# Two changes in a two-block transformer kernel: part of the mixer's convolution as diagonal matmuls, and a reordered front

## The chip, the cores and the metric

One core of one Trainium2 chip runs the whole program. The metric is the device time of one execution in microseconds (us); a lower time is better. The times shown are medians over runs of the same kernel, and one further execution was profiled.

## The reference

Two transformer blocks follow one another on 512 tokens of width 1024, all in float32. The first block has a modulation from a condition vector `c`, two attention branches of eight heads (stick breaking and forgetting) and gates. The second block adds a hybrid mixer, a cross attention to a memory of 256 rows, and a feed-forward part. What matters here is the mixer and the memory:

```python
    q, k, v, u = split(h @ w_in)                 # 512, 512, 512 and 1024 columns
    a = diff_attention(rope(q), rope(k), v)      # 4 heads, two score maps each
    a = rmsnorm(a, subln_g) * (1.0 - lam_init)
    c = u[..., :512] * sigmoid(u[..., 512:])     # the gated unit
    c = causal_dwconv(c, cv_dw_w) + cv_dw_b      # 31 taps for each of 512 channels
    c = silu(layernorm(c, cv_ln_g, cv_ln_b))
    return concat(a, c) @ w_out
    ...
    m = rmsnorm(mem, norm_mem_g)                 # 256 x 1024
    kv = m @ w_ckv                               # keys and values of the cross attention
```

## The kernel before, in words

Activations lie feature-major, 128 features on the partitions and 512 tokens along the row. Weights are stored as units of 128 x 1024 floats (512 KB). `unit` (L150) loads one on SP's queue into one of three `wr` tiles, ScalarE copies it to a rounded `wh` (L146), and VectorE or GpSimd writes the remainder `wl` (L147). Which of the two does it is set by a string: "D" is VectorE, "P" is GpSimd, and "DP" alternates. The strings are `START_LO`, `B1_LO`, `B2_LO` and so on; the list restarts at its first letter when a stage changes it. Each product is three matmuls (high times high, high times low, low times high, L153 to L156), with the moving operand 512 or 256 columns wide. `lin_k` (L158) runs one unit of eight blocks, so 24 matmuls; `tok` (L170) runs 48 matmuls of 256 columns for a unit.

PSUM has eight banks: three for `lin`, three for `z`, one for `pv` and one for `sm`.

The program is written as straight Python, but the order in which each engine gets its instructions is made by a scheduler of the framework. It takes the written order as a priority and moves work forward where its model finds an engine free and a buffer available. Every engine then works through its own queue in order, and so does each DMA queue.

**The front (L304 to L424).** `memory` (L314) loads the transposed memory (two transfers of 512 KB), scales and splits it, then loads the memory a second time by rows (`mem_n`, again two transfers of 512 KB), squares it on ScalarE with a row sum (L334), and from that makes the norm of the rows. Then a loop over eight `j` runs one unit of keys (`mem_k`, L338), two `ar` loads and multiply-sums for shift and scale (`ada`, L380, L384, 16 loads of 512 KB in four buffers), and after every second `j` two units of values (`mem_v`, L345). The four loads of `x` stand in the first pass, the norm of `x` (`row_norm`, L390) in the second: squares on ScalarE, column sums as matmuls with one column. At the end eight `h` tiles are made (L414 to L418), the inputs of all later products. The keys and values go to memory through GpSimd's DMA queue (L343, L363).

**The mixer (L760 to L1006).** The order is a string, `MIX` (L92), read at L966:

```python
MIX = "u0 u1 u2 u3 q0 f0 q1 f1 v1 v0 f3 b0 b1 c b3 f2 l b2"
```

`u` is the gated unit of 128 channels (`glu`, L768: two units of weights, products by `rb` on VectorE at L774 and L775, a sigmoid, a product on GpSimd at L777). `q` makes rotated queries and keys of two heads (`rotated`, L817, six small VectorE operations on each of two tiles, L830 to L835). `f` is the first half of a head (`diff_front`, L861: transposes at L842, scores, softmax), `b` the second (`diff_back`, L887: transposes at L492, the product with the values in `pv`, a norm). `v` makes values. `c` is the convolution of all four channel groups (`conv`, L908), `l` the layer norm (L941). For each of the four groups VectorE runs one `tensor_scalar` for tap 0 (L917) and 23 taps as `scalar_tensor_tensor` (L929), both tensor inputs in SBUF:

```python
dve.scalar_tensor_tensor(out=ca, in0=x_, scalar=w_, in1=ca, op0=ALU.mult, op1=ALU.add)
```

Seven taps go over ScalarE (a scaled copy, L922 and L925) and GpSimd (an addition, L926); L930 adds the two sums. After the mixer its output products `wo2c` (L988, the convolution's half) and `wo2a` (L996, the heads' half) follow.

Of the kernel before, what the change touches and what calls it, by code (L numbers as in the profile page):

```python
# [7 lines left out]
F32 = mybir.dt.float32  # L8
# [34 lines left out]
for _name, _n in (  # L43
# [4 lines left out]
):  # L48
    _add(_name, _n)
# [41 lines left out]
GLU_LO = "PPD"  # L91
MIX = "u0 u1 u2 u3 q0 f0 q1 f1 v1 v0 f3 b0 b1 c b3 f2 l b2"  # L92


@with_exitstack
def block_kernel(ctx, tc, wts, vec, c_row, lam_v, cst, x_t, mem_t, mem_n, pos, out):
    nc = tc.nc
# [210 lines left out]
    ms = []  # L310
    mrc = st.tile([P, 2], F32, name="mrc")
    mrb = st.tile([P, NM], F32, name="mrb")

    def memory():  # L314
        mem_r = mem_t.rearrange("(k p) m -> p k m", p=P)
        msum = st.tile([P, 2], F32, name="msum")
        for j in range(2):
            raw = st.tile([P, D], F32, tag="mr", bufs=4, name="mr")
            nc.sync.dma_start(out=raw.rearrange("p (k m) -> p k m", k=4), in_=mem_r[:, 4 * j:4 * j + 4])
            for a in range(2):  # L320
                hi, lo = htile(), htile()
                src = raw[:, a * T:(a + 1) * T]
                for e in range(2):
                    k = 4 * j + 2 * a + e
                    m = slice(e * NM, (e + 1) * NM)
                    g = V("g_mem", k)
                    act.activation(out=hi[:, m], in_=src[:, m], func=AF.Identity, scale=g)
                    dve.scalar_tensor_tensor(out=lo[:, m], in0=src[:, m], scalar=g, in1=f32(hi[:, m]),
                                             op0=ALU.mult, op1=ALU.subtract)
                    ms.append((hi[:, m], lo[:, m]))  # L330
        for i in range(2):
            raw = st.tile([P, D], F32, tag="mr", bufs=4, name="mr")
            nc.sync.dma_start(out=raw, in_=mem_n[i * P:(i + 1) * P])
            act.activation(out=raw, in_=raw, func=AF.Square, accum_out=msum[:, i:i + 1])  # L334
        rsq(mrc, msum, D)
        bcast(mrc, mrb, 2)

    def mem_k(c):  # L338
        o = ps_lin()
        lin_k(o[:, :NM], unit("mk", c), 0, ms)  # L340
        q = st.tile([P, NM], F32, tag="kvo", bufs=2, name="kvo")
        dve.tensor_tensor(out=q, in0=o[:, :NM], in1=mrb, op=ALU.mult)
        nc.gpsimd.dma_start(out=kv_d[c // 4, :, (c % 4) * NM:(c % 4 + 1) * NM], in_=q)  # L343

    def mem_v(h):  # L345
# [14 lines left out]
        for i in range(2):  # L360
            q = st.tile([P, NM], F32, tag="kvo", bufs=2, name="kvo")
            act.activation(out=q, in_=o[:, i * 256:(i + 1) * 256], func=AF.Copy, scale=mrc[:, i:i + 1])
            nc.gpsimd.dma_start(out=kv_d[2 + i, :, h * 256:(h + 1) * 256], in_=q)  # L363
# [13 lines left out]

    mod = st.tile([P, 2 * KD], F32, name="mod")

    def ada(j):  # L380
        for n, name in enumerate(("shift", "scale")):
# [6 lines left out]
                       bias=gain0[:, j:j + 1])  # L388

    def row_norm():  # L390
        cs = ps_sm()
        for k in range(KD):
            q = st.tile([P, T], F32, tag="xq", bufs=4, name="xq")
            act.activation(out=q, in_=xt0[:, k], func=AF.Square)
            for i in range(NT):
                mm(cs[:, i:i + 1], q[:, i * P:(i + 1) * P], ones[:, 0:1], k == 0 and i == 0, k == KD - 1)
        xrc = st.tile([P, NT], F32, name="xrc")
        rsq(xrc, cs[:, :NT], D)
        xrb = st.tile([P, T], F32, name="xrb")
        bcast(xrc, xrb)  # L400
        return xrb

    hs = []
    for j in range(KD):
        mem_k(j)
        if j == 0:
            for k in range(0, KD, 2):
                nc.sync.dma_start(out=xt0[:, k:k + 2], in_=x_t[k * P:(k + 2) * P].rearrange("(k p) t -> p k t", p=P))
        ada(j)
        if j == 1:  # L410
            xrb = row_norm()
        if j % 2:
            mem_v(j // 2)
    for j in range(KD):  # L414
# [3 lines left out]
        hs.append(split_sb(xk))  # L418
    csts = st.tile([P, D], F32, tag="ar", bufs=AR_BUFS, name="csts")
# [467 lines left out]
    def diff_back(h, pt, s0):  # L887
# [19 lines left out]

    def conv():  # L908
        for c in range(4):
            cp = cps[c]  # L910

            def tap(j):
                return cp[:, 30 - j:30 - j + T], V("cv_w", c * 31 + j)

            ca = b2p.tile([P, PADW], F32, tag="cp", bufs=CP_BUFS, name="ca")[:, :T]
            x_, w_ = tap(0)
            dve.tensor_scalar(out=ca, in0=x_, scalar1=w_, scalar2=V("cv_b", c), op0=ALU.mult, op1=ALU.add)  # L917
            cb_ = (rb[:, 1], nacc[:, 0])[c % 2]
            for j in range(1, 1 + CONV_POOL):
                x_, w_ = tap(j)  # L920
                if j == 1:
                    act.activation(out=cb_, in_=x_, func=AF.Copy, scale=w_)  # L922
                else:
                    pr = b2p.tile([P, T], F32, tag="cpr", bufs=2, name="cpr")
                    act.activation(out=pr, in_=x_, func=AF.Copy, scale=w_)  # L925
                    pool.tensor_tensor(out=cb_, in0=cb_, in1=pr, op=ALU.add)  # L926
            for j in range(1 + CONV_POOL, 31):
                x_, w_ = tap(j)
                dve.scalar_tensor_tensor(out=ca, in0=x_, scalar=w_, in1=ca, op0=ALU.mult, op1=ALU.add)  # L929
            dve.tensor_tensor(out=ca, in0=ca, in1=cb_, op=ALU.add)  # L930
            cacc.append(ca)
            if c == 1:
                csum.append(nacc[:, 1])
                pool.tensor_tensor(out=csum[0], in0=cacc[0], in1=ca, op=ALU.add)
            elif c == 2:
                pool.tensor_tensor(out=csum[0], in0=csum[0], in1=ca, op=ALU.add)

# [28 lines left out]
    for step in MIX.split():  # L966
# [203 lines left out]
def _layout(i):  # L1170
# [83 lines left out]
    for h in range(8):  # L1254
# [32 lines left out]
```

## Time and profile before

| | us |
|---|---|
| median of 3 runs | 1299.48 (1299.35 to 1299.97) |
| the profiled execution | 1301.97 |
| its span, from first to last instruction | 1300.0 |
| TensorE matmul busy | 1220.0 (94%) |
| TensorE weight load busy | 1035.3 (80%) |
| VectorE busy | 831.4 (64%) |
| ScalarE busy | 595.0 (46%) |
| GpSimd busy | 404.1 (31%) |

Engines: PE is TensorE's matmul, PEld its weight load, DVE VectorE, ACT ScalarE, POOL GpSimd, SP the queue that issues most DMAs. Busy shares are averages over stages with different limits. The granted clock (PEclk) is 1.00 at 2.4 GHz and 0.50 at 1.2 GHz. A line of the trace is often that of a helper, so the tile's name tells what it belongs to. Matmuls are pipelined: the mean duration of one is longer than the distance to the next, which is taken from how many start in a stretch.

### The profile page before, as it was taken

To read this page: it belongs to the slowest core of one execution; us is meant where nothing else is said; L and a number is where in the kernel's file an instruction comes from. 1 tells how busy PE (TensorE), PEld (TensorE's weight loads), DVE (VectorE), ACT (ScalarE), POOL (GpSimd) and SP (SyncE) were. 2 spreads that over 40 slices of the span, in tenths; PEclk is the share of its full clock that TensorE was granted. 3 is DMA by queue.
4 is the path that set the end of the run, shared out by engine and by line. 5 is a ranking of instruction groups with operands and counts; after the bars stand their busy time and mean duration, and the time that the engine had idled before them with its cause. 6 is when DMAs were issued, how large, how long until landed. Compare 5 with 4: busy or idle time off the path is not lost.

```text
span 1300.0 us, 16674 instructions
## 1 busy us (share of the span) xinstructions
PE 1220.0 (94%) x6310; PEld 1035.3 (80%) x6310; DVE 831.4 (64%) x1276; ACT 595.0 (46%) x985; POOL 404.1 (31%) x280
## 2 busy tenths in 40 slices
PE   6999999999999999986697799999999999999996
PEld 5899887988887888875595687887888888888886
DVE  5963777666466175699999757466587777771112
ACT  5743556456652236334445646444444444442221
POOL 0121543422221228456721018103422222223222
PEclk8999999999999999987896689999999999999998
DMA  9863232222247443221221014211333233322221
GB/s 362 287 218 99 74 98 73 66 82 89 66 138 247 139 125 109 86 65 49 73 58 41 9 49 146 83 49 56 106 98 98 97 97 98 98 89 89 92 87 65
DMA packets 43425, 134.85 MB, mean 104 GB/s; under 512 B 4945, under 2 KB 8529, under 8 KB 43346
## 3 DMA queue, kind: packets, MB, share of 16 engines
q1 hardware_dynamic: 42578, 131.69, 31.9%
q0 software_dynamic: 768, 2.10, 0.4%
q8 instruction: 50, 0.82, 0.2%
q14 instruction: 29, 0.24, 0.1%
HBM read 124.33 MB, written 6.29 MB: 100 GB/s over the span
## 4 chain that ended last, share of the span: by engine, by line
PE 77%; DVE 14%; ACT 4%; DMA 3%; issue 2%; POOL 1%; SPq 0%; DVEq 0%; ACTq 0%; POOLq 0%
PE lin L128 64%; PE z L128 6%; DVE ca L929 6%; PE pv L128 3%; DVE wl L147 1%; PE sm L128 1%; PE z L492 1%; DMA wr<-in_wts 1%; DVE h L200 1%; DVE xr L758 1%; DMA ar<-in_wts 1%; DMA wr<-kv_d 1%; ACT wh L146 0%; PE sm L237 0%; DVE h L834 0%
## 5 line engine op out<-in xcount | busy, mean ns | idle before, releaser
L128 PE MATMUL lin<-h,wh 128*128 128x512 f32 (+1 forms) x2296 | 708.9, 389 | 9.7 <-ACT wh L146 7.9
L128 PEld LDWEIGHTS lin<-h,wh 128*128 128x128 f32 x2296 | 428.7, 191 | 95.4 <-ACT wh L146 10.9
L128 PE MATMUL lin<-h,wl 128*128 128x512 f32 (+1 forms) x1148 | 444.8, 388 | 5.6 <-DVE wl L147 3.8
L147 POOL TENSOR_TENSOR wl<-wr,wh 128x1024 fp32r<-128x1024 f32 (+1 forms) x87 | 214.2, 2463 | 468.7 <-ACT wh L146 435.9
L146 ACT CAST wh<-wr 128x1024 fp32r<-128x1024 f32 (+1 forms) x193 | 200.6, 1041 | 264.7 <-PE lin L128 184.0
L128 PEld LDWEIGHTS lin<-h,wl 128*128 128x128 f32 x1148 | 219.2, 191 | 48.9 <-DVE wl L147 4.9
L147 DVE TENSOR_TENSOR wl<-wr,wh 128x1024 fp32r<-128x1024 f32 (+1 forms) x106 | 137.2, 1294 | 140.0 <-ACT wh L146 139.1
L128 PE MATMUL lin<-wh,h 128*128 128x256 f32 x672 | 133.0, 293 | 6.4 <-DVE cp L774 5.0
L128 PEld LDWEIGHTS lin<-wh,h 128*128 128x128 f32 x672 | 111.6, 201 | 6.9 <-DVE cp L774 5.2
L1110 DVE SCALAR_TENSOR_TENSOR cv<-up,vecs,cv 128x512 f32<-128x512 f32 x88 | 94.1, 1070 | 18.3 <-ACT cv L1108 16.8
L128 PE MATMUL lin<-wl,h 128*128 128x256 f32 x336 | 98.2, 293 | 0.0
L929 DVE SCALAR_TENSOR_TENSOR ca<-cp,vecs,ca 128x512 f32<-128x512 f32 x92 | 94.9, 1072 | 0.1
L128 PE MATMUL lin<-zz,wh 128*128 128x512 f32 (+1 forms) x324 | 92.4, 370 | 0.0
L128 PEld LDWEIGHTS lin<-wl,h 128*128 128x128 f32 x336 | 67.3, 200 | 0.3
L128 PEld LDWEIGHTS lin<-zz,wh 128*128 128x128 f32 x324 | 58.5, 188 | 11.4
L128 PE MATMUL lin<-zz,wl 128*128 128x512 f32 (+1 forms) x162 | 60.0, 370 | 0.0
L295 POOL TENSOR_TENSOR nacc<-nacc,sq 128x512 f32<-128x512 f32 x34 | 52.5, 1554 | 17.1 <-ACT sq L294 16.7
L1105 POOL MEMSET up<- 128x2 f32 x44 | 4.3, 99 | 148.5 <-DVE cv L1110 116.4
L563 POOL TENSOR_TENSOR zs<-zs,y 64x512 f32<-64x512 f32 x16 | 26.4, 1653 | 71.8 <-DVE y L562 69.5
L128 PE MATMUL z<-qk 128*128 128x512 f32 (+3 forms) x96 | 38.5, 401 | 5.9 <-ACT p L879 3.2
L577 DVE TENSOR_TENSOR_SCAN om<-om 128x511 f32<-128x511 f32 (+3 forms) x32 | 36.7, 1187 | 8.2 <-ACT om L573 8.0
L1117 ACT ACTIVATE cv<-cv 128x512 f32<-128x512 f32 x22 | 13.9, 632 | 59.5 <-DVE cv L1110 59.5
(355 smaller groups left out, 1639.6 us busy)
## 6 DMA issues: line engine op xcount, KB each, us to landing
wr<-in_wts SPq DMA_DIRECT2D x193, 512.0 KB, 3.5
ar<-in_wts SPq DMA_DIRECT2D x16, 512.0 KB, 6.3
qk<-qk SPq DMA_DIRECT2D x24, 128.0 KB, 2.2
wr<-in_wts SPq DMA_DIRECT2D x8, 384.0 KB, 3.0
xt<-in_x_t SPq DMA_DIRECT2D x4, 512.0 KB, 9.4
kv_d<-kvo POOLq DMA_DIRECT2D x16, 128.0 KB, 3.7
ma_d<-gt SPq DMA_DIRECT2D x8, 256.0 KB, 4.4
ma<-ma_d SPq DMA_DIRECT2D x8, 256.0 KB, 3.2
```

The source lines that it names most:

```text
L128: pe.matmul(o, lhsT=lhsT, rhs=rhs, start=start, stop=stop, skip_group_check=True)
L146: act.copy(out=hi[:, :n], in_=raw[:, :n])
L147: lo_engine().tensor_tensor(out=lo[:, :n], in0=raw[:, :n], in1=f32(hi[:, :n]), op=ALU.subtract)
L200: dve.scalar_tensor_tensor(out=lo, in0=src, scalar=g, in1=f32(hi), op0=ALU.mult, op1=ALU.subtract)
L295: pool.tensor_tensor(out=acc, in0=acc, in1=q, op=ALU.add)
L492: pe.transpose(z[:, o + i * P:o + (i + 1) * P], pt[rb_][:, ro:ro + P], ident)
L563: pool.tensor_tensor(out=zs[r], in0=zs[r], in1=y[r], op=ALU.mult)
L577: dve.tensor_tensor_scan(out=om[:, o:e], data0=om[:, o:e], data1=om[:, o:e], initial=1.0, op0=ALU.mult, op1=ALU.bypass)
L758: dve.scalar_tensor_tensor(out=xr[:, c], in0=xr[:, c], scalar=V("final_g", c), in1=rb[:, 1], op0=ALU.mult, op1=ALU.mult)
L929: dve.scalar_tensor_tensor(out=ca, in0=x_, scalar=w_, in1=ca, op0=ALU.mult, op1=ALU.add)
L1110: dve.scalar_tensor_tensor(out=r, in0=up[:, 2 - j:2 - j + T], scalar=V("ffn_w", c * 3 + j), in1=r, op0=ALU.mult, op1=ALU.add)
L1117: act.activation(out=a, in_=a, func=AF.Silu)
```

## The change

The convolution: for each group, taps 0 to 7 become eight diagonal 128 x 128 blocks of one new weight unit (`cd`, four units in all), multiplied by the padded, split input in 24 matmuls of 512 columns into the `sm` bank. VectorE adds taps 8 to 21 to that bank in place, ScalarE and GpSimd do nine taps (22 to 30) and the bias, and VectorE adds the two sums. The four groups stand apart in `MIX`, the steps of attention between them. `diff_back` takes its column sums and its broadcast in `lin` banks, since `sm` is in use.

The split of weights in the mixer moves to GpSimd (`B2_LO` from "DP" to "P"; with "PPD" restarting at each `u`, the two units of each `u` too). `QK_BUFS` goes from 7 to 6.

The front: the row copy of the memory is gone. Its norm comes from squares of the transposed tiles, three GpSimd additions and two matmuls. The order is written out (`FRONT`). `START_LO` alternates, `ar` has eight buffers, `x`'s squares are summed on GpSimd, `cb` and `xrb` stay in PSUM (the `z` and `pv` banks are opened after the front), and 6 + 8 matmuls of zeros (`spin`) are put in.

```diff
-START_LO = "D"
-AR_BUFS = 4
+START_LO = "DP"
+AR_BUFS = 8
 B1_LO = "DP"
-B2_LO = "DP"
+B2_LO = "P"
+SPIN = (6, 8)
+FRONT = ("k0 k1 n o0 o1 x0 k2 o2 x2 k3 o3 x4 x6 v0 a0 k4 o4 a1 k5 o5 r v1 a2 k6 o6 a3 k7 o7 h0 h1 a4 v2 h2 a5 a6 v3 "
+         "h3 h4 a7 h5 h6 h7")
-CONV_POOL = 7
-QK_BUFS = 7
+CONV_POOL = 9
+QK_BUFS = 6
-MIX = "u0 u1 u2 u3 q0 f0 q1 f1 v1 v0 f3 b0 b1 c b3 f2 l b2"
+MIX = "u0 q0 f0 c0 u1 q1 f1 c1 v1 v0 u2 f3 b0 c2 u3 b1 c3 b3 f2 l b2"
...
+    stp = start.enter_context(tc.tile_pool(name="stp", bufs=1, space=PSUM))
+    cb = stp.tile([P, D], F32, name="cb")
+    xrb = stp.tile([P, T], F32, name="xrb")
+    idle = stp.tile([P, T], F32, name="idle")
...
+    def spin(n):
+        for _ in range(n):
+            pe.matmul(idle, lhsT=zeros[:, :P], rhs=zeros, start=True, stop=True, skip_group_check=True)
...
-        for i in range(2):
-            raw = st.tile([P, D], F32, tag="mr", bufs=4, name="mr")
-            nc.sync.dma_start(out=raw, in_=mem_n[i * P:(i + 1) * P])
-            act.activation(out=raw, in_=raw, func=AF.Square, accum_out=msum[:, i:i + 1])
-        rsq(mrc, msum, D)
+    def memory_norm():
+        for raw in raws:
+            act.activation(out=raw, in_=raw, func=AF.Square)
+        s = raws[0]
+        pool.tensor_tensor(out=s, in0=s, in1=raws[1], op=ALU.add)
+        pool.tensor_tensor(out=s[:, :T], in0=s[:, :T], in1=s[:, T:], op=ALU.add)
+        pool.tensor_tensor(out=s[:, :NM], in0=s[:, :NM], in1=s[:, NM:T], op=ALU.add)
+        o = ps_sm()
+        for i in range(2):
+            mm(o[:, i:i + 1], s[:, i * P:(i + 1) * P], ones[:, 0:1], True, True)
+        rsq(mrc, o[:, :2], D)
         bcast(mrc, mrb, 2)
...
+            q = st.tile([P, T], F32, tag="xq", bufs=3, name="xq")
+            act.activation(out=q, in_=xt0[:, i], func=AF.Square)
+            pool.tensor_tensor(out=xacc, in0=xacc, in1=q, op=ALU.add)
...
-        dve.scalar_tensor_tensor(out=s0, in0=col_sums([aq]), scalar=1.0 / P, in1=s0, op0=ALU.mult, op1=ALU.add)
+        dve.scalar_tensor_tensor(out=s0, in0=col_sums([aq], ps_lin), scalar=1.0 / P, in1=s0, op0=ALU.mult, op1=ALU.add)
-        bcast(s0, ar)
+        bcast(s0, ar, ps_=ps_lin)
...
+    NPE = 8 * CV_UNITS
+    def conv(c):
+        cp = cps[c]
...
+        xh, xl = (b2p.tile([P, PADW], F32R, tag=t, bufs=1, name=t) for t in ("cph", "cpl"))
+        split_sb(cp, xh, xl)
+        cz = ps_sm()
+        for g in range(CV_UNITS):
+            lin_k(cz, unit("cd", CV_UNITS * c + g), 0,
+                  [(xh[:, 30 - j:30 - j + T], xl[:, 30 - j:30 - j + T]) for j in range(8 * g, 8 * g + 8)],
+                  start=g == 0, stop=g == CV_UNITS - 1)
...
+        for j in range(NPE, 31 - CONV_POOL):
+            x_, w_ = tap(j)
+            dve.scalar_tensor_tensor(out=cz, in0=x_, scalar=w_, in1=cz, op0=ALU.mult, op1=ALU.add)
+        ca = b2p.tile([P, PADW], F32, tag="cp", bufs=CP_BUFS, name="ca")[:, :T]
+        dve.tensor_tensor(out=ca, in0=cz, in1=cb_, op=ALU.add)
```

## Rows read from the trace of the kernel before

**Rows 1.** The chain of waits, whole span: start us, us, what the chain runs over
```profile
61.06 32.68 PE lin L128 x214
...
541.98 8.18 DVE xr L758 x8
...
580.07 22.55 DVE ca L929 x12
...
754.75 4.45 PE lin L128 x18
```

**Rows 2.** Windows by stage: length, busy us of engines (instructions), granted clock, DMA share, GB/s
```profile
0.00:61.00 61.00, 47.06 (x298) 43.41 (x298) 42.31 (x83) 40.11 (x75) 4.19 (x11) 0.92 0.92 333
...
84.00:200.00 116.00, 116.00 (x657) 99.09 (x657) 69.62 (x84) 58.51 (x99) 47.48 (x33) 1.00 0.33 100
...
566.00:700.00 134.00, 95.86 (x664) 89.14 (x663) 133.68 (x200) 57.19 (x110) 64.59 (x35) 0.82 0.20 64
700.00:754.80 54.80, 44.77 (x211) 36.54 (x209) 39.91 (x128) 33.12 (x76) 2.55 (x2) 0.66 0.05 10
529.00:754.80 225.80, 177.63 (x1044) 156.60 (x1043) 203.40 (x372) 103.02 (x204) 81.71 (x43) 0.81 0.17 52
```

**Rows 3.** Who waited for whom, PE, mixer (529 to 754.8): total us, times, longest
```profile
PE z L842 <- DVE h L835: 18.7, 3, 8.8
...
PE lin L128 <- DVE cp L774: 5.0, 1, 5.0
```

**Rows 4.** Windows where PE runs densely: 256 columns (585), 512 columns (1040)
```profile
585.00:590.00 5.00, 5.00 (x44) 5.00 (x43) 5.00 (x4) 1.94 (x5) 4.92 (x3) 1.00 0.29 88
...
1040.00:1060.00 20.00, 20.00 (x90) 16.57 (x89) 15.62 (x18) 7.90 (x11) 4.17 (x6) 1.00 0.33 105
```

**Rows 5.** Groups of DVE, 529 to 754.8 us
```profile
L929 DVE SCALAR_TENSOR_TENSOR ca<-cp,vecs,ca 128x512 f32<-128x512 f32 x92 | 94.9, 1072 | 0.1
L147 DVE TENSOR_TENSOR wl<-wr,wh 128x1024 fp32r<-128x1024 f32 x9 | 12.0, 1336 | 0.2 <-ACT wh L146 0.2
...
L834 DVE TENSOR_TENSOR h<-ro 128x64 f32<-128x64 f32 x8 | 6.1, 757 | 0.0
```

**Rows 6.** Timeline of the mixer, DVE and POOL beside it
```profile
572.30 4.71 DVE L929 SCALAR_TENSOR_TENSOR ca<-cp,vecs,ca 128x512 f32<-128x512 f32 x7
...
579.99 22.62 DVE L929 SCALAR_TENSOR_TENSOR ca<-cp,vecs,ca 128x512 f32<-128x512 f32 x12
...
587.40 5.14 POOL L926 TENSOR_TENSOR rb<-rb,cpr 128x512 f32<-128x512 f32 x3
```

**Rows 7.** Groups of DVE, whole span
```profile
L733 DVE SCALAR_TENSOR_TENSOR xr<-lin,mgate,xr 128x512 f32<-128x512 f32 x8 | 6.0, 745 | 9.9 <-PE lin L128 9.9
...
L833 DVE TENSOR_TENSOR ro<-h,sinb 128x64 f32<-128x64 f32 x8 | 1.7, 215 | 0.0
```

**Rows 8.** Groups of POOL, 529 to 754.8 us
```profile
L147 POOL TENSOR_TENSOR wl<-wr,wh 128x1024 fp32r<-128x1024 f32 x11 | 29.9, 2722 | 29.7 <-ACT wh L146 15.9 <-DVE ca L929 13.8
...
L926 POOL TENSOR_TENSOR rb<-rb,cpr 128x512 f32<-128x512 f32 x12 | 19.3, 1605 | 2.4 <-ACT cpr L925 1.9
L777 POOL TENSOR_TENSOR cp<-cp,sg 128x512 f32<-128x512 f32 x4 | 8.9, 2219 | 22.0 <-ACT sg L776 22.0
```

**Rows 9.** Groups of ACT, 529 to 754.8 us
```profile
L146 ACT CAST wh<-wr 128x1024 fp32r<-128x1024 f32 x19 | 19.9, 1048 | 12.3 <-issue 8.5 <-PE lin L128 3.6
L925 ACT ACTIVATE cpr<-cp,vecs 128x512 f32<-128x512 f32 x24 | 17.0, 722 | 13.4 <-POOL rb L926 6.3 <-POOL nacc L926 4.7 <-POOL cp L777 2.4
```

**Rows 10.** Groups of PE, 0 to 90 us: times, busy us, mean ns, idle before
```profile
L128 PE MATMUL lin<-h,wh 128*128 128x512 f32 x22 | 6.8, 390 | 0.0
L128 PE MATMUL lin<-h,wl 128*128 128x512 f32 x11 | 4.3, 389 | 0.0
```

**Rows 11.** Waits of SP's queue, 0 to 95 us: total us, times, longest
```profile
SPq L133 <- DVE wl L147: 27.8, 14, 3.4
```

**Rows 12.** The page's DMA rate in 40 slices of 32.5 us, GB/s
```profile
GB/s 362 287 218 99 74 98 73 66 82 89 66 138 247 139 125 109 86 65 49 73 58 41 9 49 146 83 49 56 106 98 98 97 97 98 98 89 89 92 87 65
```

More of the change, by code (lines that the diff above doesn't have):

```diff
@@ L367, in block_kernel @@
     for a in range(2):
-        o = ps_lin()
-        mm(o, ones[0:1], crow[:, a * T:(a + 1) * T], True, True)
-        act.copy(out=cb[:, a * T:(a + 1) * T], in_=o)
+        mm(cb[:, a * T:(a + 1) * T], ones[0:1], crow[:, a * T:(a + 1) * T], True, True)
+    spin(SPIN[1])
     gain0 = st.tile([P, KD], F32, name="gain0")
@@ L388, in ada, with load_x, token_h @@
                        bias=gain0[:, j:j + 1])
-    def row_norm():
[L391 to L396, printed above, removed]
-        xrc = st.tile([P, NT], F32, name="xrc")
[L398 to L414, printed above, removed]
+    def load_x(k):
+        nc.sync.dma_start(out=xt0[:, k:k + 2], in_=x_t[k * P:(k + 2) * P].rearrange("(k p) t -> p k t", p=P))
+        for i in (k, k + 1):
+            if i == 0:
+                act.activation(out=xacc, in_=xt0[:, 0], func=AF.Square)
+                continue
+            q = st.tile([P, T], F32, tag="xq", bufs=3, name="xq")
+            act.activation(out=q, in_=xt0[:, i], func=AF.Square)
+            pool.tensor_tensor(out=xacc, in0=xacc, in1=q, op=ALU.add)
+    def row_norm():
+        xrc = st.tile([P, NT], F32, name="xrc")
+        rsq(xrc, col_sums([xacc]), D)
+        bcast_mm(xrc, xrb)
+    def token_h(j):
         xk = xt0[:, j]
@@ L418, in block_kernel @@
         hs.append(split_sb(xk))
+    hs, ko = [], {}
+    for step in FRONT.split():
+        n = int(step[1:] or 0)
+        if step[0] == "k":
+            ko[n] = mem_k(n)
+        elif step[0] == "o":
+            mem_k_out(n, ko.pop(n))
+        elif step[0] == "v":
+            mem_v(n)
+        elif step[0] == "x":
+            load_x(n)
+        elif step[0] == "a":
+            ada(n)
+        elif step[0] == "h":
+            token_h(n)
+        elif step[0] == "n":
+            memory_norm()
+        elif step[0] == "r":
+            row_norm()
     csts = st.tile([P, D], F32, tag="ar", bufs=AR_BUFS, name="csts")
@@ L424, in block_kernel @@
     start.close()
+    psz = ctx.enter_context(tc.tile_pool(name="psz", bufs=1, space=PSUM))
     ROWS = (((0, 0),), ((1, 0), (3, 384)), ((2, 0),))
@@ L905, in block_kernel @@
     cacc, csum = [], []
[L908 to L936, printed above, removed]
@@ new lines, in block_kernel, with tap @@
+    NPE = 8 * CV_UNITS
+    def conv(c):
+        cp = cps[c]
+        def tap(j):
+            return cp[:, 30 - j:30 - j + T], V("cv_w", c * 31 + j)
+        xh, xl = (b2p.tile([P, PADW], F32R, tag=t, bufs=1, name=t) for t in ("cph", "cpl"))
[5 more added lines that the diff above has]
+                  start=g == 0, stop=g == CV_UNITS - 1)
+        cb_ = (rb[:, 1], nacc[:, 0])[c % 2]
+        for j in range(31 - CONV_POOL, 31):
+            x_, w_ = tap(j)
+            if j == 31 - CONV_POOL:
+                act.activation(out=cb_, in_=x_, func=AF.Identity, scale=w_, bias=V("cv_b", c))
+            else:
+                pr = b2p.tile([P, T], F32, tag="cpr", bufs=2, name="cpr")
+                act.activation(out=pr, in_=x_, func=AF.Copy, scale=w_)
+                pool.tensor_tensor(out=cb_, in0=cb_, in1=pr, op=ALU.add)
+        for j in range(NPE, 31 - CONV_POOL):
+            x_, w_ = tap(j)
+            dve.scalar_tensor_tensor(out=cz, in0=x_, scalar=w_, in1=cz, op0=ALU.mult, op1=ALU.add)
+        ca = b2p.tile([P, PADW], F32, tag="cp", bufs=CP_BUFS, name="ca")[:, :T]
+        dve.tensor_tensor(out=ca, in0=cz, in1=cb_, op=ALU.add)
+        cacc.append(ca)
+        if c == 1:
+            csum.append(nacc[:, 1])
+            pool.tensor_tensor(out=csum[0], in0=cacc[0], in1=ca, op=ALU.add)
+        elif c == 2:
+            pool.tensor_tensor(out=csum[0], in0=csum[0], in1=ca, op=ALU.add)
@@ L1200, in _layout @@
     pc["u2"] = cols(w_in2[:, 1536:])
+    cd = np.zeros((4, CV_UNITS, P, 8, P), np.float32)
+    w = i["cv_dw_w_2"][0].reshape(31, 4, P)
+    for k in range(8 * CV_UNITS):
+        cd[:, k // 8, np.arange(P), k % 8, np.arange(P)] = w[k]
+    pc["cd"] = cd.reshape(-1, P, D)
     for j, n in enumerate(["q2", "k2", "v2"]):
```

36 lines of the change are left out of this document (21 added, 15 removed), and 1 row of the table N_UNITS.

## The prediction

> **What bounds the kernel now.** I read the chain of waits first. It runs over PE nearly everywhere, and only two stretches leave it for long: the front, up to 61 us, where PE waits for loads and VectorE, and the mixer, where from 542 us the chain runs on VectorE, first on `xr`, then on the convolution's taps, one piece of twelve taps alone lasting 22.55 us; it is back on PE for good with `wo2c` at 754.75 us [rows 1]. The windows say the same in busy time. In the front PE is busy 47 of 61 us, while the DMA engines are 92% busy at 333 GB/s. From 84 to 200 us PE is busy throughout, so what the front gains is handed on. In the mixer's middle, 566 to 700 us, VectorE is busy 133.7 of 134 us and PE 95.9; in its tail, 700 to 754.8 us, neither is full and the granted clock falls to 0.66 [rows 2]. What PE waits for is VectorE's queue: rotated heads 18.7 us, the glu's product 5.0 us [rows 3].
>
> So the path is PE's work plus PE's slack, stage by stage, and the rest of the kernel (84 to 529 us, and after 755 us) is left as it is.
>
> **The mixer, PE.** From 529 us (first `u` matmuls) to 754.8 us are 225.8 us, with PE busy 177.6, so 48 idle. The clock adds to that: 0.66 in the tail means 68% of its time at the half level; of 44.8 busy us some 30 ran there and lost 15. In the middle 0.82 means 36% of 134 us, which I take as half idle: 24 busy us, 12 lost [rows 2]. Slack 48 + 27 = 75 us, work at full clock 151 us.
>
> *Added:* 4 groups x 24 = 96 matmuls of 512 columns; 90 of them start in 20 us, 0.222 us each [rows 4]: 21.3 us on PE, on the path in full. Work afterwards 172 us.
>
> **The mixer, VectorE.** 92 taps cost 94.9 us busy, 1.07 us each [rows 5]. That mean hides two speeds: seven taps in 4.71 us (0.67 each) while GpSimd is mostly quiet, and twelve in 22.6 us (1.88 each) while GpSimd adds without a pause, 1.71 us an addition [rows 6]. Afterwards 56 taps remain, now with one tensor input in SBUF and the other, as the result, in PSUM. No row shows an operation of VectorE writing PSUM. Bounds: 0.67 us (the quiet taps) and 1.88 us (the blocked ones), [rows 6]. I take 0.745 us, from the same instruction with an input in PSUM and GpSimd at work in that stage [rows 7]: 56 x 0.745 = 41.7 us. The Trainium skill, page "SBUF — State Buffer", section "Who interferes with whom", says that a VectorE instruction with two SBUF inputs and a GpSimd instruction that reads SBUF lock each other out for a whole instruction, and that one with at most one SBUF input doesn't take part; the two speeds in [rows 6] agree with the first half. By it the taps would be free of GpSimd, and it speaks against the change elsewhere (below).
> The nine remainders of weights that VectorE made, 12.0 us, leave it [rows 5]; four splits of the padded input come, 0.75 each by [rows 7], 3 us; the four `tensor_scalar` and four additions I hold even. VectorE's load: 203.4 [rows 2] - 94.9 - 12.0 + 41.7 + 3 = 141 us, of some 206: no longer full.
>
> **The mixer, the others.** GpSimd: all 24 units' remainders now, 2.72 us each, 65 us; 32 additions instead of 24 at 1.6 us, 51 us; four glu products 8.9 us [rows 8]: 125 us against 81.7 [rows 2]. ScalarE: four casts at 1.05, eight products more and four copies at 0.72 [rows 9], 13 us on 103 [rows 2]. SP: four loads of 512 KB, 2.1 MB, 6 us at the front's rate, with DMA 17% busy in this stage [rows 2]; the heads' copies of `k` (two per head) now stand on SP among weight loads that wait for a free `wr`, and one held there holds its head's scores, at worst for one unit of PE, 5.5 us, beside other work. `sm` is held for a whole group, so groups can't overlap; with 14 taps of 0.745, 10.4 us a group, they needn't. The moved column sums take a `lin` bank for a few us per head, and `QK_BUFS` 6 lets the next head's first two tiles in only after the scores of the last: a few us at worst, inside the slack below.
>
> **The mixer's slack afterwards.** Middle: 38 idle + 12 lost = 50 us. With VectorE at two thirds of its time instead of all of it I keep a third, 16 us. Tail: 10 + 15 = 25 us. The new order spreads `u2`, `u3`, `c2` and `c3` between the heads, but the last group's taps (10.4 us) and the layer norm still end on the path; I keep 18 us. Slack 34, stage 172 + 34 = 206 us, **20 us less**. Bounds: slack 21 (only the tail's chain and a few gaps: 33 us less) and 75 (nothing gained: 21 us more).
>
> **The front.** Before, 33 matmuls of 512 columns had started by 90 us [rows 10], at 0.222 [rows 4] 7.3 us: the first block's products began near 82.7 us, and that is when the memory's work was through. Afterwards 38 loads of 512 KB remain of 40, with the small ones 20.3 MB; at 333 GB/s [rows 2] they are in at 61 us. Then the last unit's cast 1.05 [rows 9], remainder 2.7 [rows 8] and 24 matmuls of 256 columns at 0.114 [rows 4], 2.7: 67.5, and 2 us for queues: 69.5. PE's own need, 384 x 0.114 = 44 us, fits before that. **13 us less.** What makes room is not the dropped 1.05 MB (3.1 us at this rate) but that SP waited 27.8 us in all for VectorE to free `wr` [rows 11]: half of the remainders go to GpSimd, `ar` has eight buffers, and `ada` reads `cb` from PSUM. The 14 spin matmuls lie where PE is idle and cost nothing; if weights were there already they would cost 6 us at 0.44 each, twice the full-clock distance [rows 4]. GpSimd's seven additions of squares, three of the memory and eight remainders are some 36 us at [rows 8]'s prices and are hidden behind loads; its queue also issues the stores of keys and values, which wait for results, and a remainder behind such a store waits too. Bounds: 3.1 us (bytes alone) and 20 us (362 GB/s, the page's first slice [rows 12], gives 56 + 6.5 = 62.5).
>
> **Sum.** The profiled execution took 1301.97 us with a span of 1300.0; 1301.97 - 20 - 13 = 1269; the median of the runs lies 2.5 lower, so I forecast 1266.5 us.
>
> **Rivals.**
> (a) *Front hidden by DMA.* If the 92% is a limit and the order of PE's work doesn't matter, only the bytes count: 3.1 instead of 13, 1276.4 us. For it: the DMA share [rows 2]. Against: the backlog of 21 us on PE after the loads end.
> (b) *PSUM doesn't free the taps.* At 1.88 us [rows 6] 56 taps cost 105 us, VectorE's load is 204 us as before, the stage stays at 226 us and only the front gains: 1286.5 us. For it: no row of a write to PSUM. Against: 0.745 in [rows 7] beside a busy GpSimd.
> (c) *Slower.* GpSimd takes VectorE's place in the mixer. Its 125 us over 24 units are 5.2 us a unit, and PE needs 24 x 0.222 = 5.3 or 48 x 0.114 = 5.5 [rows 4]: no reserve where work is dense. The small rotary operations, 0.215 us undisturbed and 0.757 in their worst place [rows 5, 7], pay beside it. If the slack stays 75, PE's extra 21.3 us stand against the front's 13: 1307.8 us. It decides from a slack of 67 on. By the lock that the Trainium skill describes (same page and section) each of the 48 rotary operations could wait for half a remainder of 2.72 us, 65 us in all, and VectorE would be back at 206 us. Against: remainders are made ahead, into three buffers.
> (d) *Both at their best:* 33 + 20, 1246.5 us.
>
> **How the numbers follow.** Forecast 60% (its own range 1253 to 1279), (a) 12%, (b) 11%, (c) 8%, (d) 9%. 1246 to 1287 leaves out (c), part of (d) and the far side of (b). A measurement tells 0.2% (2.6 us) from nothing: slower 7%, the same 3% (the edge of (c) and of (b)), faster 90%.
>
> **What would show it.** Right: taps in PSUM near 0.75 us even beside GpSimd; VectorE some 140 us busy between the first `u` and `wo2c`, that stage near 206 us; the first block's products starting near 70 us. Wrong: taps well over 1 us (b); PE's waits for `wl` by GpSimd, and rotary operations near 1 us (c); loads ending at 61 us with PE still behind by 20 us (a). A stage after the mixer that changes by more than 3 us would make the whole split wrong.

## The result, and the profile after

The changed kernel takes **1315.44 us** (median of 4 runs, 1313.01 to 1316.98); the kernel before, timed beside it, 1299.72 (1299.35 to 1303.81). The ratio is 1.0112, 95% interval 1.0086 to 1.0138: **slower by 1.1%, where 2.5% faster (1266.5 us) was forecast**, and outside the range of 1246 to 1287 us. Its profiled execution has a span of 1314.0 us.

The chain of waits after (start us, us, what) answers to [rows 1]:

```profile
56.12 41.24 PE lin L134 x286
97.36 6.47 PE z L134 x54
...
690.52 6.64 PE lin L134 x22
697.52 7.33 PE lin L134 x34
...
767.38 25.40 PE lin L134 x103
```

The chain enters a z bank of block one at 97.36 us (before: 93.74) and reaches the mixer's output products at 767.4 us (before: 754.75) [rows 1]. What follows the first of these products takes 546.4 us, 545.2 before. So against this one profile of the kernel before the front lost some 3.6 us and the mixer 10, and nothing else moved by more than 1.2.

Where in the mixer? Its windows after, cut at 660 us, and below them cut at 700 us, where [rows 2] is cut (columns as there):

```profile
532.05:660.00 127.95, 118.95 (x821) 108.44 (x820) 107.58 (x169) 64.98 (x119) 68.91 (x40) 0.99 0.28 83
660.00:767.65 107.65, 70.49 (x321) 55.25 (x322) 74.54 (x174) 58.22 (x112) 34.53 (x25) 0.76 0.10 30
532.05:767.65 235.60, 189.44 (x1142) 163.69 (x1142) 182.12 (x343) 123.20 (x230) 103.43 (x64) 0.88 0.20 59
...
532.05:700.00 167.95, 148.71 (x953) 132.24 (x953) 133.64 (x226) 86.12 (x162) 85.82 (x52) 0.94 0.24 71
700.00:767.65 67.65, 40.74 (x191) 31.46 (x190) 48.48 (x118) 37.07 (x69) 17.61 (x12) 0.74 0.09 28
```

and the kernel before, cut at the same time:

```profile
529.00:660.00 131.00, 101.44 (x626) 92.67 (x626) 123.62 (x163) 50.65 (x80) 71.73 (x38) 0.87 0.20 63
660.00:754.75 94.75, 76.14 (x419) 63.88 (x417) 79.73 (x210) 52.32 (x124) 9.98 (x5) 0.73 0.13 37
```

Up to 660 us the change does what was forecast: PE is busy 93% of the time at a clock of 0.99, where it was busy 77% at 0.87. Then the gain is given back: fewer matmuls are left (321 against 419), and they take 107.7 us instead of 94.8, PE idle for 37 of them (19 before). VectorE isn't full there either (74.5 of 107.7). No engine is busy throughout; something waits in line.

The groups of VectorE in the mixer after answer to [rows 5]; the last two are the softmax's weighted difference (L924; L883 before) and a rotary operation (L876; L835 before):

```profile
L976 DVE SCALAR_TENSOR_TENSOR sm<-cp,vecs,sm 128x512 f32<-128x512 f32 x56 | 42.0, 749 | 0.6
...
L924 DVE SCALAR_TENSOR_TENSOR p<-p,smc 128x512 f32<-128x512 f32 (+3 forms) x16 | 14.8, 928 | 0.2
...
L876 DVE TENSOR_TENSOR h<-ro 128x64 f32<-128x64 f32 x8 | 10.6, 1326 | 0.0
```

The mean of L876 hides two speeds, as its shortest, median and longest times in ns show; the taps have only one. Below them is one of the long ones, beside a remainder on GpSimd that takes as long:

```profile
L876 DVE TENSOR_TENSOR h<-ro x8: 211/1326/2443, 552.5 to 617.1; 128x64 f32<-128x64 f32 x8
L976 DVE SCALAR_TENSOR_TENSOR sm<-cp,vecs,sm x56: 734/751/758, 572.7 to 741.5; 128x512 f32<-128x512 f32 x56
...
562.50 2.41 POOL L153 TENSOR_TENSOR wl<-wr,wh 128x1024 fp32r<-128x1024 f32 x1
562.55 2.44 DVE L876 TENSOR_TENSOR h<-ro 128x64 f32<-128x64 f32 x1
```

What waits for what at the end of the mixer can be followed on PE and VectorE in the changed kernel. Head 0's column sums, its broadcast and the last gated unit, on PE:

```profile
677.92 1.05 PE L243 MATMUL lin<-ones,aq 128*128 128x1 f32 x8 [1.17 <-ACT aq L937]
...
690.52 0.48 PE L134 MATMUL lin<-identr,bch 128*128 128x128 f32 x1 [0.85 <-ACT bch L282]
690.80 1.16 PE L134 MATMUL lin<-h,wh 128*128 128x512 f32 x2
...
712.49 0.79 PE L134 MATMUL sm<-cph,wh 128*128 128x512 f32 x1 [1.22 <-ACT cph L198]
...
724.83 0.39 PE L134 MATMUL pv<-th,v2h 128*128 128x512 f32 x1
...
767.38 0.47 PE L134 MATMUL lin<-identr,bch 128*128 128x128 f32 x1 [4.87 <-ACT bch L282]
767.65 1.16 PE L134 MATMUL lin<-h,wh 128*128 128x512 f32 x2
```

and VectorE in between, where the steps of the reciprocal root (`rq`, 0.15 us each) take turns with taps:

```profile
686.41 0.15 DVE L269 TENSOR_TENSOR rq<-rq 128x4 f32<-128x4 f32 x1
686.54 0.76 DVE L976 SCALAR_TENSOR_TENSOR sm<-cp,vecs,sm 128x512 f32<-128x512 f32 x1
687.20 0.15 DVE L270 SCALAR_TENSOR_TENSOR rq<-rq 128x4 f32<-128x4 f32 x1
687.33 0.76 DVE L976 SCALAR_TENSOR_TENSOR sm<-cp,vecs,sm 128x512 f32<-128x512 f32 x1
...
742.88 0.68 DVE L978 TENSOR_TENSOR ca<-sm,nacc 128x512 f32<-128x512 f32 x1
...
767.26 0.69 DVE L199 TENSOR_TENSOR h<-ca,h 128x512 fp32r<-128x512 f32 x1 [0.77 <-ACT h L198]
```

From head 0's sums to its broadcast 12.6 us pass; the last gated unit stands behind that broadcast in PE's queue and starts at 690.8 us. So the last group's diagonal products begin at 712.5, the third head's product with the values stands right behind them (724.83), the group's sum is made at 742.88, and the layer norm and the last head's broadcast reach the end **together**, at 767.3 us.

### The profile page after: what moved, and what is told of

It is laid out like the page before. It is cut to its first block, busy times and chain, and to the rows that moved or that the text cites. A ratio compares the mean times of both kernels' runs of the same rounds, so it can differ in the third digit from the quotient of the medians.

```text
span 1314.0 us, 16828 instructions
## 1 busy us (share of the span) xinstructions
PE 1229.4 (94%) x6368; PEld 1036.9 (79%) x6368; DVE 803.5 (61%) x1221; ACT 611.8 (47%) x1001; POOL 472.1 (36%) x322
## 4 chain that ended last, share of the span: by engine, by line
PE 76%; DVE 13%; ACT 4%; issue 3%; DMA 2%; POOL 2%; SPq 0%; DVEq 0%; POOLq 0%; ACTq 0%
PE lin L134 66%; PE z L134 5%; DVE sm L976 2%; PE pv L134 2%; DVE wl L153 1%; PE z L533 1%; DMA wr<-in_wts 1%; DVE ar L413 1%; ACT wh L152 1%; DVE p L924 1%; DVE h L206 1%; POOL wl L153 1%; DVE nm L919 0%; PE sm L134 0%; ACT cpr L972 0%
## 5 line engine op out<-in xcount | busy, mean ns | idle before, releaser
L153 POOL TENSOR_TENSOR wl<-wr,wh 128x1024 fp32r<-128x1024 f32 (+1 forms) x110 | 268.0, 2436 | 484.0 <-ACT wh L152 455.2
L152 ACT CAST wh<-wr 128x1024 fp32r<-128x1024 f32 (+1 forms) x197 | 204.9, 1042 | 276.5 <-PE lin L134 207.8
L153 DVE TENSOR_TENSOR wl<-wr,wh 128x1024 fp32r<-128x1024 f32 (+1 forms) x87 | 115.6, 1328 | 139.8 <-ACT wh L152 139.0
L134 PE MATMUL lin<-wh,h 128*128 128x256 f32 x672 | 128.4, 288 | 2.0 <-ACT wh L152 1.1
L134 PEld LDWEIGHTS lin<-wh,h 128*128 128x128 f32 x672 | 108.0, 195 | 2.6 <-ACT wh L152 1.4
L976 DVE SCALAR_TENSOR_TENSOR sm<-cp,vecs,sm 128x512 f32<-128x512 f32 x56 | 42.0, 749 | 0.6
```

Source lines behind the costliest of these rows:

```text
L134: pe.matmul(o, lhsT=lhsT, rhs=rhs, start=start, stop=stop, skip_group_check=True)
L152: act.copy(out=hi[:, :n], in_=raw[:, :n])
L153: lo_engine().tensor_tensor(out=lo[:, :n], in0=raw[:, :n], in1=f32(hi[:, :n]), op=ALU.subtract)
L976: dve.scalar_tensor_tensor(out=cz, in0=x_, scalar=w_, in1=cz, op0=ALU.mult, op1=ALU.add)
```

## The experiments

Two marks are read from each trace. *z* is the start of block one's first matmul into a z bank (the expectations call these the score matmuls). *Stage* runs from the first column sum of the norm ahead of the mixer to the first output product: 227.4 us before, 237.4 in the changed kernel. The marks are better than totals: between them lies a stretch that no kernel changes and that took 429 to 436 us in the profiled executions. Each ratio is to the kernel before as timed beside that kernel (medians of 1299.7 to 1303.7 us), not to the first row. Where no ratio stands, a kernel ran once.

| kernel | z | stage | us | ratio to before |
|---|---|---|---|---|
| before | 93.6 | 227.4 | 1299.7 | |
| changed | 97.2 | 237.4 | 1315.4 | 1.0112 (1.0086 to 1.0138) |
| front_only | 97.6 | 227.7 | 1311.8 | 1.0075 (1.0055 to 1.0096) |
| mixer_only | 97.7 | 238.6 | 1316.0 | 1.0106 (1.0077 to 1.0135) |
| mix_early | 98.3 | 232.0 | 1313.8 | 1.0091 (1.0061 to 1.0121) |
| lo_dp | 97.9 | 233.5 | 1312.5 | 1.0083 (1.0056 to 1.0109) |
| u3_up | 98.0 | 231.8 | 1314.3 | 1.0100 (1.0078 to 1.0123) |
| u3_up_dp | 99.2 | 231.1 | 1310.5 | 1.0067 (1.0046 to 1.0089) |
| l_up | 98.6 | 230.1 | 1309.6 | 1.0048 (1.0025 to 1.0070) |
| spread | 97.9 | 253.9 | 1331.6 | 1.0222 (1.0188 to 1.0256) |
| spread_dp | 98.4 | 248.2 | 1328.5 | 1.0192 (1.0154 to 1.0231) |
| no_norm | 96.4 | 235.6 | 1311.8 | |
| ar4 | 92.8 | 238.3 | 1309.1 | |
| no_norm_ar4 | 92.2 | 234.6 | 1304.9 | |
| no_diag | 98.6 | 225.9 | 1308.4 | |
| no_taps23 | 98.7 | 233.6 | 1315.2 | |
| no_headnorm | 99.0 | 225.5 | 1299.9 | |
| conv_first | 99.2 | 223.6 | 1301.3 | 1.0003 (0.9990 to 1.0016) |
| conv_first_ar4 | 93.1 | 220.5 | 1294.6 | 0.9939 (0.9915 to 0.9962) |
| f2_up | 93.1 | 219.2 | 1295.5 | 0.9942 (0.9921 to 0.9963) |

**Each part alone.** `front_only` has the old mixer, `mixer_only` the old front.

> The changed front with the mixer of before (whole convolution on VectorE, old order, remainders alternating, seven taps on GpSimd, seven tiles of queries and keys). Theory, that the two parts add up and that the new front costs 3 to 4 us by its order: 1302 to 1304 us, first products of block one near 97 us as in the changed kernel, mixer near 226 us. Rival, that the front's 13 us are there but are lost to what the new mixer does to the stages behind it: 1286 to 1290 us.

> The front of before with the changed mixer. Theory: the mixer alone costs 10 to 12 us, 1309 to 1313 us, first products of block one near 94 us. Rival, that the old mixer's stage is only late because of what came before it: 1295 to 1300 us.

The mixer's loss stays with the mixer (238.6 us with the old front, 227.7 with the old mixer). The front's is less plain. By the totals the new front costs 10 us beside the old mixer (1311.8, and 1301.6 for the kernel before timed with it) and nothing beside the new one (ratio 1.0112 with the new front, 1.0106 with the old), so the parts don't add up in the totals as the theory had it. By the marks, the old front came to z at 97.7 us here, against 93.6 in the profile of before, at a lower granted clock, as the window 0 to 97 us of `mixer_only` shows:

```profile
0.00:97.00 97.00, 82.44 (x509) 77.03 (x510) 63.53 (x110) 55.36 (x96) 11.87 (x22) 0.88 0.79 277
```

(0.93 in the profile of before). The old front scatters by 4 us between these two profiles; the new one came at 97.2 to 99.2 us in all thirteen profiles that have it unchanged, the old one's late end. The total of `front_only`, 1311.8, is above the expected 1302 to 1304. Its own profiled execution took 1307.18, with 549.3 us behind the mixer where before had 545.2; where the rest went isn't settled.

**Another order, other remainders.** Order and `B2_LO` of the changed kernel, one at a time:

```diff
-MIX = "u0 q0 f0 c0 u1 q1 f1 c1 v1 v0 u2 f3 b0 c2 u3 b1 c3 b3 f2 l b2"
+MIX = "u0 u1 c0 u2 c1 u3 q0 f0 c2 q1 f1 v1 v0 f3 c3 b0 b1 b3 f2 l b2"   # mix_early
+B2_LO = "DP"                                                            # lo_dp
```

> The changed kernel with another order of the mixer: all four gated units and the first three groups of the convolution stand ahead of or between the first heads, the last group before the first second half of a head, so that the layer norm has two heads and f2 beside it. Theory, that the changed kernel's order puts the last group and the layer norm alone at the end: the stage falls from 235 us to 205 to 220, the time to 1285 to 1300 us. Rival, that GpSimd's queue with all remainders and nine taps a group sets the pace: stage still 230 to 240, 1310 to 1318 us. Second rival, that the banks (one sm for a whole group, lin shared with the heads' norms) hold the work: the same 1310 to 1318 us, with the waits for lin and sm grown.

> The changed kernel with the mixer's remainders of queries, keys, values and diagonals alternating between VectorE and GpSimd, as before the change. Rival, that GpSimd's queue paces the mixer: 1295 to 1305 us. Theory, that the order of the work does: within 4 us of the changed kernel, 1311 to 1319 us.

5.4 and 3.9 us off the stage. `mix_early` (232.0 us) fell into the range of its two rivals, though not for the first one's reason: `lo_dp` (1312.5 us) fell into the range of its theory, that GpSimd's queue doesn't set the pace. GpSimd alone for the remainders is worth 3.9 us of the stage here, and 0.7 and 5.7 in the two pairs below. The early order paid at the other end: the first half of head 0 came only at 632 us (580 in the changed kernel).

**The last gated unit, the layer norm, the heads.**

```diff
-MIX = "u0 q0 f0 c0 u1 q1 f1 c1 v1 v0 u2 f3 b0 c2 u3 b1 c3 b3 f2 l b2"
+MIX = "u0 q0 f0 c0 u1 q1 f1 c1 v1 v0 u2 u3 f3 b0 c2 b1 c3 b3 f2 l b2"   # u3_up
+MIX = "u0 q0 f0 c0 u1 q1 f1 c1 v1 v0 u2 u3 f3 b0 c2 b1 c3 l b3 f2 b2"   # l_up
+MIX = "u0 q0 f0 c0 v0 u1 f1 b0 c1 u2 b1 q1 c2 u3 f3 v1 c3 f2 b3 l b2"   # spread
```

(`u3_up_dp`, `l_up` and `spread_dp` with alternating remainders.)

> The changed kernel with one step of the mixer's order moved: the last gated unit stands right behind the third one, ahead of the first second half of a head, instead of behind it. In the changed kernel its products start at 690.5 us, behind the norm of head 0 in PE's queue. Theory, that the last group is late because of that place: its products start by 670 us, the taps of the last group end by 715 us instead of 742, the stage falls from 235 us to 212 to 222, the time to 1292 to 1303 us. Rival, that the heads' own chains of small operations fill the tail whatever stands between them: the taps end earlier but the stage stays at 228 to 236 us, 1308 to 1316 us.

> The same order, and the mixer's remainders alternating between VectorE and GpSimd as before the change. Theory: the 4 us that the alternation gave with the other order come on top, 1288 to 1299 us. Rival (the heads' chains fill the tail): 1304 to 1312 us.

> The changed kernel with the last gated unit moved up, the alternating remainders, and the layer norm ahead of b3 and f2 in the order. There the last group's sum was ready at 720 us, but the layer norm's first subtraction came at 737 us. Theory, that the layer norm's place in PE's queue cost these 15 us and that its output products can then fill PE beside the last heads: 8 to 20 us less than with the layer norm in its old place, 1288 to 1302 us. Rival, that the last head's second half ends the stage anyway: 1304 to 1311 us.

> The changed kernel with another order of the mixer alone: the values of heads 0 and 1 are made before queries and keys of heads 2 and 3, so that the second halves of heads 0 and 1 stand among the units, and the last gated unit and the last groups of the convolution stand before f3 and f2. New theory, from the moved gated unit: PE's units are done by 660 us as predicted, but the four second halves of the heads, each a string of small dependent operations, still stand behind them in the order and run to 750 us with PE mostly idle; spread among the units they cost little: stage 205 to 220 us instead of 237, time 1284 to 1299 us. Rival, that the strings of small operations are delayed by VectorE's taps wherever they stand: stage 228 to 240 us, 1307 to 1318 us.

> The same order with the mixer's remainders alternating between VectorE and GpSimd. Theory: 2 to 4 us less than with GpSimd alone, 1281 to 1297 us. Rival: 1303 to 1315 us.

In `u3_up` the last sum was made at 727.3 us instead of 742.9, but the stage fell by 5.6 only, into the rival's range: the last head's product with the values came at 747.6 us, 749.1 in the changed kernel (the stage starts 2.9 us later in `u3_up`, so these are 18.5 and 4.4 us earlier in it). That is what two strings that end together look like: mending one shows the other. The same holds for `l_up`: its layer norm moved up gave 1.0 us of stage over `u3_up_dp`, which differs in nothing else, where 8 to 20 were expected. `spread` is the miss that taught most. Its heads 0 and 1 were through early (products with the values at 622 and 650 us), but heads 2 and 3 came at 748 and 766, and the middle was no longer dense:

```profile
567.00:660.00 93.00, 68.17 (x338) 57.14 (x338) 65.45 (x128) 42.77 (x83) 38.23 (x25) 0.79 0.18 56
```

A second half of a head among the units holds the units behind it: in this window PE waited 8.6 us for steps of the second halves (`tl` and `aq`), and in the changed kernel for none of them. That accounts for a part of the 25 idle us; the rest wasn't followed. My theory that the second halves cost little there fell, and its rival's range was left on the far side.

**What the tail consists of.** Three kernels leave a part of the changed one out.

> The changed kernel without the diagonal products: taps 0 to 7 of every group are left out, with their weight unit, the split of the input and the 96 matmuls; VectorE's first tap starts the sum. The prediction put 21.3 us on the path in full for them. Theory of the prediction: the stage falls from 237 us to 212 to 217. Theory now, that the stage is paced by strings of dependent operations in its last third, and that the dense part only fills what would be idle: 226 to 234 us, and VectorE's taps of a group start earlier.

> The changed kernel without VectorE's taps of the last two groups (taps 8 to 21 of groups 2 and 3 are left out, 28 operations, 21 us). Theory, that these taps stand in VectorE's queue between the steps of the heads' norms and softmaxes and so stretch the end: the stage falls by 12 to 25 us, to 212 to 225. Rival, that the heads' strings are long by themselves, each step waiting for the one before on another engine: it falls by at most 6 us, 231 to 238.

> The changed kernel without the twelve small operations of each head's reciprocal root (the row factor is left as it comes out of the sum). Theory, that the heads' norm strings, interleaved with taps, hold PE's queue at the broadcast: stage 10 to 20 us less, 217 to 227. Rival, that the broadcast's place doesn't matter because the tail waits for the last group and the softmax of the last head: at most 5 us less, 232 to 238.

Without the diagonal products (with their weights and the split of the input) the stage is 11.5 us shorter, half of the 21.3 that were put on the path in full; the prediction's range fell, and 225.9 us lies at the edge of the newer theory's. Without 21 us of VectorE's taps in the last two groups it is 3.8 us shorter, in the rival's range. That doesn't clear the taps: counted from the stage's start the last sum is made 18 us earlier (at 194.8 us, not 212.7), but the last head's product with the values only 4.5 us (at 214.4, not 218.9), so the other of the two strings now ends the stage. Without the 48 operations of the reciprocal roots, 0.15 us each when undisturbed, it is 11.9 us shorter, and what follows the mark another 3.9: they are short, but each waits its turn, and PE's queue stands behind the last one. From head 0's sums to its broadcast 12.6 us pass in the changed kernel, 6.6 without those taps and 2.3 without the roots.

**The convolution ahead of the heads.** All four groups before the first second half, alternating remainders, the rest as changed:

```diff
+MIX = "u0 q0 f0 c0 u1 q1 f1 c1 u2 u3 c2 v1 v0 f3 c3 b0 b1 l b3 f2 b2"
+B2_LO = "DP"
```

> The changed kernel with alternating remainders and an order in which all groups of the convolution stand ahead of every second half of a head: u2, u3, c2, then the values, f3, c3, then the heads. Theory, that taps among the heads stretch the end: stage 212 to 224 us, time 1290 to 1301 us. Rival, that the heads' strings need the same time wherever the taps stand: stage 229 to 236, 1306 to 1313 us.

223.6 us, at the theory's edge: 13.8 us less than the changed kernel, 9.9 of it by the order (`lo_dp` has the same remainders). The last group's sum is made at 694.6 us, and the windows show PE dense up to 660 us and a shorter tail:

```profile
530.00:660.00 130.00, 125.99 (x808) 111.93 (x808) 119.87 (x186) 76.88 (x133) 67.38 (x44) 0.99 0.28 84
660.00:752.27 92.27, 69.71 (x347) 59.38 (x345) 64.46 (x170) 48.05 (x100) 19.34 (x13) 0.68 0.11 32
```

**The front.** `no_norm` replaces the memory's norm by ones, `ar4` goes back to four buffers, `no_norm_ar4` does both.

```diff
-AR_BUFS = 8
+AR_BUFS = 4
```

> The changed kernel with the memory's norm left out: its sums are still made, but the row scales are set to one, so the first keys needn't wait for them. Theory, that the late norm holds the three lin banks and with them PE from 24 to 33 us: PE has no hole there, and the first products of block one (in the changed kernel at 97.4 us by the score matmuls) come 5 to 9 us earlier, 88 to 92 us. Rival, that the order of the loads sets the front (shift and scale weights ahead of the key weights on SP's queue): the hole moves, the first products stay at 95 to 98 us.

> The changed kernel with four instead of eight buffers for the shift and scale weights, so that fewer of these loads run ahead of the key weights. Theory of the late norm: no gain, the score matmuls of block one start at 96 to 99 us as in the changed kernel. Rival (order of the loads): the key weights come earlier, 89 to 94 us.

> The changed kernel with the memory's norm left out (row scales set to one) and four buffers for the shift and scale weights. Theory, that late norm and order of the loads hide one another: the score matmuls of block one start at 84 to 89 us. Rival, that the norm costs nothing once the loads are in order: 91 to 94 us, as with four buffers alone.

The theory of the late norm fell: 0.8 us alone, 0.6 more with four buffers. The rival held: four buffers bring z from 97.2 to 92.8 us (92.2 to 93.1 in all four profiles with four, 97.2 to 99.2 in the thirteen with eight). SP's queue in the changed kernel, where all eight buffers are filled before the next weights of the keys:

```profile
7.17 10.63 SPq L412 DMA_DIRECT2D ar<-in_wts  x8
18.77 0.33 SPq L641 DMA_DIRECT2D lamt<-in_lam  x1
20.11 2.87 SPq L139 DMA_DIRECT2D wr<-in_wts  x3
23.93 8.39 SPq L412 DMA_DIRECT2D ar<-in_wts  x8
37.82 0.81 SPq L139 DMA_DIRECT2D wr<-in_wts  x2
```

and in `ar4`:

```profile
7.44 4.46 SPq L412 DMA_DIRECT2D ar<-in_wts  x4
12.86 0.33 SPq L641 DMA_DIRECT2D lamt<-in_lam  x1
14.19 4.82 SPq L139 DMA_DIRECT2D wr<-in_wts  x3
...
48.31 4.68 SPq L412 DMA_DIRECT2D ar<-in_wts  x3
```

The shift and scale weights came sooner, all sixteen issued by 32.3 us instead of 53.0, but not the loads as a whole: from 24 to 56 us the changed kernel moved 293 GB/s, and PE was busy 16.7 of 32 us,

```profile
24.00:56.00 32.00, 16.66 (x94) 15.29 (x94) 30.32 (x58) 17.56 (x36) 12.73 (x12) 0.68 0.74 293
```

and in `ar4` 331, with PE busy 22.3 us and 166 matmuls instead of 94:

```profile
24.00:56.00 32.00, 22.32 (x166) 21.91 (x166) 24.93 (x49) 16.09 (x31) 18.31 (x16) 0.84 0.90 331
```

SP's queue isn't the only place where weights wait there. Two weights whose loads were issued at 37.8 and 38.2 us landed within 7.7 us, but in the changed kernel PE waits until 53.3 us for the cast of the first of them and until 56.1 for its remainder. VectorE works through `ar`'s sums until 50.06 us, then through `x` (`xt`), and only then makes that remainder; ScalarE's cast stands behind steps that wait for the same sums and for `xt`. The next weights are issued at 56.09 us:

```profile
50.06 4.87 DVE L436 TENSOR_TENSOR xt<-xt,xrb 128x512 f32<-128x512 f32 x8
53.34 0.80 PE L134 MATMUL lin<-h,wh 128*128 128x256 f32 x2 [4.06 <-ACT wh L152]
54.84 1.22 DVE L153 TENSOR_TENSOR wl<-wr,wh 128x1024 fp32r<-128x1024 f32 x1
56.09 5.28 SPq L139 DMA_DIRECT2D wr<-in_wts  x3
56.12 0.58 PE L134 MATMUL lin<-h,wl 128*128 128x256 f32 x1 [1.97 <-DVE wl L153]
```

So the early loads also put their sums ahead of the weights' splits. That is read from the trace; `ar4` shows the buffers' effect as a whole and doesn't part the two.

**Both mended.** `conv_first_ar4` is `conv_first` with four buffers; `f2_up` has `b0 f2 b1 l b3 b2` at the end instead of `b0 b1 l b3 f2 b2`.

> The order with the whole convolution ahead of the heads' second halves, alternating remainders, and four buffers for the shift and scale weights. Theory, that the two parts add: block one's score matmuls at 92 to 95 us instead of 99, stage 222 to 226 us, time 1295 to 1299 us. Rival, that what the front gains is lost again before the mixer or within the noise of the runs: 1299 to 1304 us.

> The same with f2 ahead of b1, so that the last head's scores don't come at 711 us, 26 us after the first second half. Theory, that the tail is the string from b0 over f2 to b2: stage 4 to 10 us less than with f2 in its old place, 214 to 220 us, time 1287 to 1295 us. Rival, that f2 waits for its tiles until other heads are through: stage 222 to 228 us.

The parts add: apart they took 14.2 and 6.3 us off the changed kernel's time, together 20.9, to 1294.56 us, ratio 0.9939, the first version faster than both kernels. `f2_up` gained 1.3 us of stage over it, inside the theory's range but not by its 4 to 10 us, and the totals can't be told apart. Its windows show what remains, PE dense to 660 us and 82 us of tail with PE busy 60:

```profile
525.00:660.00 135.00, 130.97 (x862) 117.31 (x862) 123.91 (x196) 80.44 (x139) 72.31 (x47) 1.00 0.29 84
660.00:742.46 82.46, 59.71 (x288) 49.21 (x288) 58.08 (x159) 43.95 (x93) 14.17 (x10) 0.70 0.10 30
```

## Why the prediction was wrong, step by step

- **Taps in PSUM: right.** 0.745 us forecast, 0.749 measured, 42.0 us for 56; rival (b) falls. By the Trainium skill's "SBUF — State Buffer", section "Who interferes with whom", an instruction with at most one SBUF input, outside the modes that use two ports, keeps clear of GpSimd; the trace agrees: the nine taps that ran with GpSimd busy beside them nearly throughout had a mean of 0.752 us, the longest of all 56 took 0.758.
- **PE's work: right.** The windows above give 46.2 us idle (9.0 and 37.2) and, worked out as in the prediction, some 18 lost at half clock (1 and 17): 171 us remain of 235.6; 172 were forecast.
- **The middle's slack: right up to 660 us.** To there PE idles 9.0 us and loses about 1, so 10; 16 were forecast, but for a middle that ends at 700. With that cut it idles 19 us and loses some 8: 27.
- **The tail's slack: the step that failed.** "I keep 18 us": behind 660 us 37.2 idle and 17 lost at half clock make 54, behind 700 us 27 and some 9 make 36. The prediction saw that taps and layer norm end on the path, but priced them as two strings of known length on empty queues. The change had put them into the same queues as the heads, u3 behind b0's broadcast, b3 behind c3, so that they ran one after the other. The slack as a whole was 64 us instead of 34, and these 30 us are the whole miss of the stage (235.6 against 206). Cut at 700 us, 18 of them lie in the tail; cut at 660, all of them, and the middle even gave 6 back.
- **VectorE's load: wrong, 182.1 us against 141.** The bound for the rotary operations was named in rival (c) and left out of the sum. The row L876 measures 1.326 us where the worst of these rows had 0.757 [rows 5]; all 48 take 37.4 us instead of 19.0. The softmax's `p` and `smc` rows go from 15.2 to 21.9. These have both inputs in SBUF, and the Trainium skill's page named above has such operations locked out by those of GpSimd that read SBUF; the trace agrees, 0.21 us for L876 alone and 2.4 beside GpSimd. Together they make 25 of the 41 us. But it was not the pace: alternating remainders gave 3.9 us back.
- **Rival (c)** came nearest by its time (1307.8) but not by its cause: no wait of PE for `wl` stands in its list for the mixer. Of its two signs only the other showed, rotary operations above 1 us. The slack of 64 us stayed under the 67 from which it decides; the kernel is slower all the same because the front gave nothing.
- **The front: the 13 us didn't come.** Block one's first product started at 86.3 us (82.7 before), where 70 was forecast. The eight buffers of `ar`, one of the three things that were to make room, took it. The bytes fell as forecast, but PE still waited, because one queue carries both kinds of weights in order and the sums of the early ones stand ahead of the splits of the others. Even with four buffers z comes only 0.8 us ahead of the profile of before, and 4.9 ahead of `mixer_only`, not 13; what holds the rest wasn't found.
- **Added matmuls "on the path in full":** 11.5 of 21.3 us, by `no_diag`.
- **Work after the mixer unchanged: right,** within 1.2 us.

The mixer's miss is not all accounted for by mended orders: the best stage, 219.2 us, is 8.2 under the stage before and still above the forecast, which by this mark is 207 (20 under 227.4). The 82 us after 660 that remain I put down to the strings of the heads; no run shows that, nor that they can be shortened further.

## What to carry to other kernels

When an edit relieves an engine in the dense part of a stage, work out the part that comes after it anew: list what stands behind what in each queue there, and let no two strings of small dependent operations share a queue in series. A deeper buffer also changes what a queue carries first; check whose loads, and whose work behind the loads, are pushed back. Where two strings end together, an experiment on one of them shows little, and only an order that moves both tells.

## What was not expected of the hardware

- Twelve operations a head, 14 us of VectorE by their rows in all, were worth 11.9 us of the stage, while 21 us of taps were worth 3.8.
- The same front, code unchanged, reached its mark at 93.6 us in one execution and at 97.7 in another, at a granted clock of 0.93 and 0.88.
- In `spread` PE was busy 68.2 us from 567 to 660 us, with a granted clock of 0.79, where the changed kernel had 84.7 us and 0.98: with the holes came a lower clock for the work that was left.
- A rotary operation of 0.21 us took 2.4 us beside a GpSimd operation of 2.4 us, while taps that accumulate in PSUM kept their 0.75 us.
